# First stage of a decoder trunk: c as one row spread by TensorE, the square root's table behind the squares, whole modulation rows, diagonals scaled on ScalarE

## The chip, the cores and the metric

The kernel runs on one core of a Trainium2 chip. The metric is the device time of one execution in microseconds (us), as the median of several runs. PE is TensorE, DVE is VectorE, ACT is ScalarE, POOL is GpSimd; SP issues most of the DMAs and computes nothing. SBUF is the memory that the engines work on, PSUM the one that PE writes sums into.

## The reference

One layer of a hybrid decoder trunk on x (512 tokens, 1024 features). All its modulation vectors come from one vector c:

```python
cond = jax.nn.silu(c)
mod = (cond @ w_ada[l] + b_ada[l])[:, None, :]
sh1, sc1, g1, sh2, sc2, g2 = jnp.split(mod, 6, axis=-1)
h = _rms(x, norm1_w[l]) * (1 + sc1) + sh1
x = x + g1 * _hybrid_mixer(h, w_in[l], ...)
h = _rms(x, norm2_w[l]) * (1 + sc2) + sh2
x = x + g2 * (jnp.square(jax.nn.relu(h @ w_ff1[l])) @ w_ff2[l])
```

`_hybrid_mixer` multiplies h by `w_in` (queries, keys, values, state-space inputs, pooling inputs, gates), runs dilated window attention, a chunked state-space scan and a multi-scale pooling, projects and gates the three, and multiplies by `w_out`. `_rms` divides by the root of the mean square over the features.

## The kernel before

x is held transposed: `xT[k]`, k from 0 to 7, has 128 features on the partitions and 512 tokens along them. A float32 product of matrices is made as three matmuls (`mm3`, lines 287 to 289) of parts: every operand is a high part (`hh`, `wh`) rounded to fp32r, and a low part (`hl`, `wl`), the rest. The high part of a weight is a copy on ACT, the low part a subtraction on DVE.

The first stage, which the change rewrites, is in an order written out by hand for DVE, ACT, PE and SP: each engine runs its instructions in the order in which the code calls them. What follows after the k loop of this stage is ordered by a scheduler by priorities. The stage does this:

- SP loads c, broadcast to all 128 partitions (`crow`, two halves of 512), then the eight `xT`, with `vec` (all small vectors) behind the first and a constant behind the second, then rows of the modulation's weights (`ada_load(part, k)`: two DMAs of 128x512) and of the weights of queries and keys (`w_load`).
- ACT takes the silu of `crow`, loads the table of the square root (L359) and squares `xT` (L400, L401). DVE adds the squares in pairs (L405), all but the last pair; PE sums over partitions with a matrix of ones into `sx` (L403, L406). Meanwhile `warm` keeps PE running on ones (L394).
- DVE multiplies `sx` with the identity and sums (L416), so that each token's sum of squares comes to a partition; ACT takes a root, DVE the reciprocal and one Newton step (L421 to L426): r. Four diagonal matrices with r (L430) and a matmul with ones each (L431) spread r over partitions again, in PSUM.
- `dot(k, i, half)` is a modulation value as a product of a row of weights with `crow`, multiplied and summed by one DVE instruction (L368, in the trace with a read of the accumulator behind it); `dot_end` adds bias and norm weight (L374, L375, L377). i = 0 is the scale, i = 1 the shift; `bsc` is the bias plus one (L409).
- `high(k)` makes u = xT x scale x r (L453 for k = 0; ACT L450 and DVE L451 from k = 1) and hh = u + shift (ACT L454); `low(k)` makes hl (DVE L459). `by_residue` writes hh and hl in another order of tokens (ACT L445).
- A loop over k makes 24 matmuls of queries and keys with hh and hl of k, while DVE and ACT prepare k + 1. `w_high` (ACT L383) and `w_low` (DVE L387) split the weights.

All blocks of 128x512 come from one set of 59 places (`blk`, `free`). `background` holds the other 32 rows of the modulation, each computed later at a tick of the weight stream; they use `crow` too. The weights of the later stages come through `wstream`, whose raw, high and low blocks have pools of their own (`raws`, `wsp`).

Of the kernel before, what the change touches and what calls it, by code (L numbers as in the profile page):

```python
# [17 lines left out]
P = 128  # L18
D = 1024
T = 512  # L20
# [3 lines left out]
NBLK = 59  # L24
WARM = (18, 12, 6)
AHEAD = 300
# [72 lines left out]
def kernel(ctx: ExitStack, tc: tile.TileContext, a: dict, out: bass.AP, dbg=None):  # L99
# [41 lines left out]
    def small(shape, name, bufs=1, dt=F32):  # L141
        return sm.tile(shape, dt, tag=name, name=uid(name), bufs=bufs)
# [31 lines left out]
    vec = small([P, NVCOLS], "vec")  # L174
    small([P, 464], "gap")
    crow = [blk("crow") for _ in range(2)]
    xT = [blk(f"xT{k}") for k in range(8)]
# [76 lines left out]
    def tick(n=1):  # L254
        ticks[0] += 1
        for _ in range(n):
            if side:
                side.pop(0)()
        if ticks[0] % 2 == 0 and background:
            background.pop(0)()  # L260
            if not background:
                free(*crow)

# [69 lines left out]
    E = mybir.EngineType  # L333
    with tc.manual_schedule(engines={E.DVE, E.Activation, E.PE, E.SP}):
        for i in range(2):
            nc.sync.dma_start(crow[i], a["c"][:, i * T : (i + 1) * T].broadcast_to([P, T]))
        wt = {}

        def w_load(k):
            for ch in (Q, K):  # L340
                wt[ch, k] = blk("wst")
                nc.sync.dma_start(wt[ch, k], w_in[ch, k // 2][:, k % 2, :])

        for k in range(8):
            nc.sync.dma_start(xT[k], a["x"][k])
            if k == 0:
                nc.sync.dma_start(vec, a["vec"])
            if k == 1:
                nc.sync.dma_start(cst[:, :P], a["const"][:, :P])
        wa = [ada_load(1, 0)]  # L350
        wa.append(ada_load(0, 0))
        w_load(0)
# [3 lines left out]
        S.activation(junk1, epsc, AF.Silu)  # L356
        for i in range(2):
            S.activation(crow[i], crow[i], AF.Silu)
        S.activation(junk1, epsc, AF.Sqrt)  # L359
        A1 = [small([P, 2], f"A1{k}") for k in range(8)]  # L360
        bsc1 = small([P, 8], "bsc1")
        dots = {}

        def dot(k, i, half):
            if (k, i) not in dots:
                dots[k, i] = small([P, 2], "dot", 4)
            x = wa[i][half]
            V.scalar_tensor_tensor(x, x, 1.0, crow[half], ALU.mult, ALU.mult, accum_out=dots[k, i][:, half : half + 1])  # L368
            free(x)

        def dot_end(k, i):
            d, o = dots[k, i], A1[k][:, i : i + 1]
            if i == 0:
                V.scalar_tensor_tensor(o, d[:, 0:1], bsc1[:, k : k + 1], d[:, 1:2], ALU.add, ALU.add)  # L374
                V.tensor_tensor(o, o, vc("norm1_w", k), ALU.mult)  # L375
            else:
                V.scalar_tensor_tensor(o, d[:, 0:1], vc("b_ada", k), d[:, 1:2], ALU.add, ALU.add)  # L377

        wparts = {}
# [15 lines left out]

        warm(WARM[0])
        sp = psm("sx")
        for k in range(0, 8, 2):
            s0, s1 = blk("sq"), blk("sq")
            S.activation(s0, xT[k], AF.Square)  # L400
            S.activation(s1, xT[k + 1], AF.Square)  # L401
            if k == 6:
                mm(sp, lhsT=ones, rhs=s0, start=False, stop=False)  # L403
            else:
                V.tensor_tensor(s1, s0, s1, ALU.add)  # L405
            mm(sp, lhsT=ones, rhs=s1, start=(k == 0), stop=(k == 6))  # L406
            free(s0, s1)
            if k == 0:
                V.tensor_scalar(bsc1, vc("b_ada", 8, 8), 1.0, None, ALU.add)  # L409
        dot(0, 0, 0)  # L410
        dot(0, 0, 1)
        dot_end(0, 0)
        ss, var, rt, r, t = (small([P, 4], "rx" + n) for n in "svryt")
# [4 lines left out]
        S.activation(rt, ss, AF.Sqrt, scale=1.0 / D, bias=epsc)  # L418
        w_high(Q, 0)
        w_high(K, 0)  # L420
        V.tensor_scalar(var, ss, 1.0 / D, EPS, ALU.mult, ALU.add)  # L421
        dot(0, 1, 0)
        V.reciprocal(r, rt)
# [5 lines left out]
        for b in range(4):  # L429
            V.tensor_scalar(dg[b], ident, r[:, b : b + 1], None, ALU.mult)  # L430
            mm(rp[:, b * P : (b + 1) * P], lhsT=ones, rhs=dg[b], start=True, stop=True)  # L431
        warm(WARM[2])
        R1 = blk("R1")
        dot(0, 1, 1)
        dot_end(0, 1)
        hh = [cpool.tile([P, T], F32R, name=f"hh{k}", tag=f"hh{k}") for k in range(8)]
# [29 lines left out]
        low(0)  # L466
        w_low(K, 0)
        free(rp, wps)
        qps = [acc() for _ in range(4)]
        kps = [acc() for _ in range(4)]  # L470
        for k in range(8):
            if k < 7:
                wa = [ada_load(1, k + 1), ada_load(0, k + 1)]
                w_load(k + 1)
                dot(k + 1, 0, 0)
                if k:
                    low(k)
                dot(k + 1, 0, 1)
                w_high(Q, k + 1)
                w_high(K, k + 1)  # L480
                by_residue(1, k)
                dot(k + 1, 1, 0)
                dot_end(k + 1, 0)
                dot(k + 1, 1, 1)
                w_low(Q, k + 1)
                dot_end(k + 1, 1)
                high(k + 1, R1)
                w_low(K, k + 1)
# [800 lines left out]
```

## Time and profile before

| | us |
|---|---|
| median of 3 runs (1109.05 to 1109.62) | 1109.58 |
| the profiled execution | 1109.32 |
| span of the trace in it | 1107.5 |
| PE busy | 1098.5 |
| DVE busy | 597.1 |
| ACT busy | 507.5 |

The span goes from the first to the last instruction that the profile records; the profiled execution's own time is 1.8 us longer. TensorE's granted clock is shown as full almost everywhere. A row of the timeline names the start and the busy time of a group of equal instructions, the engine, the line, output and inputs, and in brackets how long the engine was idle before and what released it. Ends of matmuls are modelled, so a row of several matmuls is a little longer than their distance times their number.

### The profile page before, as it was taken

Reading aid. Unit: us, or ns where it says so; the run is one execution under the profiler, and the core shown is the slowest. Engines: PE = TensorE matmul, PEld = TensorE weight load, DVE = VectorE, ACT = ScalarE, POOL = GpSimd, SP = SyncE. Lnnn points to the kernel's source line nnn. Section 1 sums busy time; section 2 is a strip of 40 time slices with the busy share of each in tenths; the row PEclk is TensorE's granted clock in tenths of the full one; section 3 lists DMA queues with packets and bytes.
Section 4 is the critical chain, followed back from the end, with each engine's and each line's share of the span. In section 5 each row is a group of like instructions: output and inputs, shape, how many; then the busy total and the mean of one; then the engine's idle time right before and its main releaser. Section 6 shows DMA issues by size and latency. Waiting matters only on the chain.

```text
span 1107.5 us, 14079 instructions
## 1 busy us (share of the span) xinstructions
PE 1098.5 (99%) x5414; PEld 916.5 (83%) x5414; DVE 597.1 (54%) x1210; ACT 507.5 (46%) x953; POOL 0.2 (0%) x4
## 2 busy tenths in 40 slices
PE   8999999999999999999999999999999999999998
PEld 6878888888887888888888888899888888888887
DVE  6964773574766778478832433665544223455241
ACT  6895885643596456425422223343433122344120
POOL 0000000000000000000000000000000000000000
PEclk9999999999999999999999999999999999999999
DMA  9943343444543453322323432440133222222241
GB/s 337 314 141 106 115 157 100 133 134 130 186 130 96 125 163 121 119 83 77 123 96 124 143 95 96 142 163 2 60 105 100 96 95 95 96 96 95 95 133 38
DMA packets 49348, 134.45 MB, mean 121 GB/s; under 512 B 5617, under 2 KB 6385, under 8 KB 49281
## 3 DMA queue, kind: packets, MB, share of 16 engines
q1 hardware_dynamic: 47696, 130.81, 36.4%
q10 hardware_dynamic: 1584, 2.75, 0.8%
q8 instruction: 42, 0.69, 0.3%
q14 instruction: 26, 0.20, 0.1%
HBM read 131.41 MB, written 2.13 MB: 121 GB/s over the span
## 4 chain that ended last, share of the span: by engine, by line
PE 89%; ACT 4%; DMA 4%; DVE 2%; issue 1%; SPq 0%; ACTq 0%; DVEq 0%
PE psacc L287 27%; PE psacc L289 27%; PE psacc L288 27%; DMA wa<-in_w_ada_dram 1%; PE psS L566 1%; DMA M<-prow 1%; ACT wh L272 1%; PE psy L880 1%; PE pso L682 1%; PE psyo L888 1%; PE pso L680 1%; DVE conv L798 1%; DMA wst<-in_w_in_dram 0%; PE pskT L550 0%; PE pspT L663 0%
## 5 line engine op out<-in xcount | busy, mean ns | idle before, releaser
L273 DVE TENSOR_TENSOR wl<-raw,wh 128x1024 fp32r<-128x1024 f32 x161 | 196.9, 1223 | 335.5 <-ACT wh L272 333.9
L272 ACT CAST wh<-raw 128x1024 fp32r<-128x1024 f32 x161 | 168.9, 1050 | 365.5 <-PE psacc L288 321.4
L287 PE MATMUL psacc<-hl,wh 128*128 128x512 f32 x416 | 166.4, 400 | 0.6 <-ACT prev L843 0.5
L289 PE MATMUL psacc<-hh,wl 128*128 128x512 f32 x416 | 162.3, 390 | 0.0
L288 PE MATMUL psacc<-hh,wh 128*128 128x512 f32 x416 | 162.1, 390 | 0.0
L287 PEld LDWEIGHTS psacc<-hl,wh 128*128 128x128 f32 x416 | 78.2, 188 | 18.3 <-issue 1.2
L288 PE MATMUL psacc<-ah,wh 128*128 128x512 f32 (+1 forms) x242 | 92.1, 381 | 0.0
L288 PEld LDWEIGHTS psacc<-hh,wh 128*128 128x128 f32 x416 | 78.2, 188 | 16.8 <-issue 1.4
L287 PE MATMUL psacc<-al,wh 128*128 128x512 f32 (+1 forms) x242 | 92.1, 381 | 0.0
L289 PE MATMUL psacc<-ah,wl 128*128 128x512 f32 (+1 forms) x242 | 92.0, 380 | 0.0
L289 PEld LDWEIGHTS psacc<-hh,wl 128*128 128x128 f32 x416 | 78.1, 188 | 16.6
L288 PE MATMUL psacc<-gh,wh 128*128 128x512 f32 x224 | 87.2, 389 | 0.0
L287 PE MATMUL psacc<-gl,wh 128*128 128x512 f32 x224 | 87.2, 389 | 0.0
L289 PE MATMUL psacc<-gh,wl 128*128 128x512 f32 x224 | 87.0, 389 | 0.0
L287 PE MATMUL psacc<-wl,rh 128*128 128x512 f32 x192 | 77.1, 402 | 0.0
L289 PE MATMUL psacc<-wh,rl 128*128 128x512 f32 x192 | 75.2, 392 | 0.0
L288 PE MATMUL psacc<-wh,rh 128*128 128x512 f32 x192 | 74.9, 390 | 0.0
L237 DVE SCALAR_TENSOR_TENSOR wa<-wa,crow 128x512 f32<-128x512 f32 x64 | 43.3, 688 | 19.3 <-DMA wa<-in_w_ada_dram 19.0
L287 PEld LDWEIGHTS psacc<-al,wh 128*128 128x128 f32 x242 | 45.5, 188 | 8.9
L288 PEld LDWEIGHTS psacc<-ah,wh 128*128 128x128 f32 x242 | 45.5, 188 | 8.7
L289 PEld LDWEIGHTS psacc<-ah,wl 128*128 128x128 f32 x242 | 45.5, 188 | 8.7
L287 PEld LDWEIGHTS psacc<-gl,wh 128*128 128x128 f32 x224 | 42.1, 188 | 8.7
(350 smaller groups left out, 1955.8 us busy)
## 6 DMA issues: line engine op xcount, KB each, us to landing
raw<-in_w_in_dram SPq DMA_DIRECT2D x80, 512.0 KB, 3.5
raw<-in_w_ff_dram SPq DMA_DIRECT2D x64, 512.0 KB, 3.5
wa<-in_w_ada_dram SPq DMA_DIRECT2D x96, 256.0 KB, 4.1
wst<-in_w_in_dram SPq DMA_DIRECT2D x16, 256.0 KB, 5.4
M<-prow SPq DMA_DIRECT2D x16, 256.0 KB, 3.3
raw<-in_w_ssd_out_dram SPq DMA_DIRECT2D x8, 512.0 KB, 3.5
raw<-in_w_pool_out_dram SPq DMA_DIRECT2D x8, 512.0 KB, 3.4
raw<-in_w_out_dram SPq DMA_DIRECT2D x8, 512.0 KB, 3.5
```

The lines of the kernel that those rows point to most:

```text
L237: V.scalar_tensor_tensor(wa[i], wa[i], 1.0, crow[i], ALU.mult, ALU.mult, accum_out=d[:, i : i + 1])
L272: S.copy(wh, raw)
L273: V.tensor_tensor(wl, raw, wh.bitcast(F32), ALU.subtract)
L287: mm(ps, lhsT=wh, rhs=xl, start=first, stop=False)
L288: mm(ps, lhsT=wh, rhs=xh, start=False, stop=False)
L289: mm(ps, lhsT=wl, rhs=xh, start=False, stop=last)
L566: mm(so[b], lhsT=qT[:, b * P : (b + 1) * P], rhs=kT[:, (b + 1) * P - n : (b + 1) * P], start=True, stop=True)
L680: mm(od, lhsT=vs[kb][:, hs], rhs=pT[b // 2][:, cs : cs + P], start=(b == 0), stop=False, skip_group_check=True)
L682: mm(ov[:, b, :], lhsT=vs[b][:, hs], rhs=pT[0][:, b * P : (b + 1) * P], start=False, stop=(gi == 2 and b == 3), skip_group_check=True)
L798: V.scalar_tensor_tensor(t[:, i:], x[:, : T - i], cw[:, 3 - i, n : n + 1], t[:, i:], ALU.mult, ALU.add)
L880: mm(yp[half * 64 : half * 64 + 64, cs], lhsT=X[c][:, (2 * j + half) * 64 : (2 * j + half + 1) * 64], rhs=Ms[half][:, cs], start=True, sto ...
L888: mm(op[:, cs], lhsT=prev[c][:, j * P : (j + 1) * P], rhs=CT[:, cs], start=True, stop=True)
```

## The change

- c comes as two rows on one partition (`c1`), by DMAs on ACT's queue. ACT takes the silu of a row, PE spreads it with a matmul of one row of ones into PSUM, DVE copies it to `crow2`, which has a place of its own.
- SP issues all eight `xT` first, then `vec` and the constant, then whole rows of the modulation's weights (`ada_whole`, one DMA of 128x1024) into blocks that belong to `raws` and `wsp`.
- The table of the square root is loaded behind the squares. All four pairs of squares are added on DVE, so that there are four matmuls into `sx` instead of five. `bsc` stands ahead of the additions. There are 13 instead of 18 warming matmuls at the start.
- `dot(0, 0)` is put around the diagonals in two halves, `dot_end(0, 0)` and both halves of `dot(0, 1)` behind r. The diagonals are scaled on ACT (L441). The high parts of the first weights stand behind them.
- In the k loop a `dot` is one DVE instruction on 128x1024 and one that adds and multiplies. `high(k+1)` stands right behind `dot(k+1, 1)`, and both `w_low` behind that.

```diff
-WARM = (18, 12, 6)
+WARM = (13, 12, 6)
...
-    small([P, 464], "gap")
-    crow = [blk("crow") for _ in range(2)]
+    small([P, 432], "gap")
+    crow2 = small([P, 2, T], "crow")
+    crow = [crow2[:, i, :] for i in range(2)]
...
+        c1 = [blk("c1") for _ in range(2)]
         for i in range(2):
-            nc.sync.dma_start(crow[i], a["c"][:, i * T : (i + 1) * T].broadcast_to([P, T]))
+            nc.scalar.dma_start(c1[i][:1], a["c"][:, i * T : (i + 1) * T])
...
+        homes = [(raws, "raw"), (wsp, "wh"), (wsp, "wl")]
+
+        def ada_whole(part, k):
+            pool, tag = homes[0]
+            homes.append(homes.pop(0))
+            w = pool.tile([P, 2, T], F32, tag=tag, name=uid("wada"))
+            nc.sync.dma_start(w, a["w_ada"][part * 8 + k].rearrange("p (i t) -> p i t", i=2))
+            return w
+
         for k in range(8):
             nc.sync.dma_start(xT[k], a["x"][k])
-            if k == 0:
-                nc.sync.dma_start(vec, a["vec"])
-            if k == 1:
-                nc.sync.dma_start(cst[:, :P], a["const"][:, :P])
-        wa = [ada_load(1, 0)]
-        wa.append(ada_load(0, 0))
+        nc.sync.dma_start(vec, a["vec"])
+        nc.sync.dma_start(cst[:, :P], a["const"][:, :P])
+        wa = [ada_whole(1, 0), ada_whole(0, 0)]
         w_load(0)
...
-        for i in range(2):
-            S.activation(crow[i], crow[i], AF.Silu)
-        S.activation(junk1, epsc, AF.Sqrt)
...
+        def dot(k, i):
+            w, o, d = wa[i], A1[k][:, i : i + 1], small([P, 1], "dot1", 4)
+            V.scalar_tensor_tensor(w, w, 1.0, crow2, ALU.mult, ALU.mult, accum_out=d)
+            if i == 0:
+                V.scalar_tensor_tensor(o, d, bsc1[:, k : k + 1], vc("norm1_w", k), ALU.add, ALU.mult)
+            else:
+                V.tensor_tensor(o, d, vc("b_ada", k), ALU.add)
...
         warm(WARM[0])
+        cps = [psm("c") for _ in range(2)]
+        for i in range(2):
+            S.activation(c1[i][:1], c1[i][:1], AF.Silu)
+            mm(cps[i], lhsT=ones[:1], rhs=c1[i][:1], start=True, stop=True)
+            V.tensor_copy(crow[i], cps[i])
+        free(*cps, *c1)
+        V.tensor_scalar(bsc1, vc("b_ada", 8, 8), 1.0, None, ALU.add)
         sp = psm("sx")
...
-            if k == 6:
-                mm(sp, lhsT=ones, rhs=s0, start=False, stop=False)
-            else:
-                V.tensor_tensor(s1, s0, s1, ALU.add)
+            V.tensor_tensor(s1, s0, s1, ALU.add)
             mm(sp, lhsT=ones, rhs=s1, start=(k == 0), stop=(k == 6))
             free(s0, s1)
-            if k == 0:
-                V.tensor_scalar(bsc1, vc("b_ada", 8, 8), 1.0, None, ALU.add)
-        dot(0, 0, 0)
-        dot(0, 0, 1)
-        dot_end(0, 0)
+        S.activation(junk1, epsc, AF.Sqrt)
+        dot_half(0, 0, 0)
...
         S.activation(rt, ss, AF.Sqrt, scale=1.0 / D, bias=epsc)
-        w_high(Q, 0)
-        w_high(K, 0)
         V.tensor_scalar(var, ss, 1.0 / D, EPS, ALU.mult, ALU.add)
-        dot(0, 1, 0)
+        dot_half(0, 0, 1)
...
         for b in range(4):
-            V.tensor_scalar(dg[b], ident, r[:, b : b + 1], None, ALU.mult)
+            S.mul(dg[b], ident, r[:, b : b + 1])
             mm(rp[:, b * P : (b + 1) * P], lhsT=ones, rhs=dg[b], start=True, stop=True)
         warm(WARM[2])
+        dot_end(0, 0)
+        dot_half(0, 1, 0)
+        dot_half(0, 1, 1)
+        dot_end(0, 1)
+        w_high(Q, 0)
+        w_high(K, 0)
         R1 = blk("R1")
-        dot(0, 1, 1)
-        dot_end(0, 1)
...
         low(0)
-        w_low(K, 0)
...
             if k < 7:
-                wa = [ada_load(1, k + 1), ada_load(0, k + 1)]
+                wa = [ada_whole(1, k + 1), ada_whole(0, k + 1)]
                 w_load(k + 1)
-                dot(k + 1, 0, 0)
+                dot(k + 1, 0)
                 if k:
                     low(k)
-                dot(k + 1, 0, 1)
+                else:
+                    w_low(K, 0)
                 w_high(Q, k + 1)
                 w_high(K, k + 1)
                 by_residue(1, k)
-                dot(k + 1, 1, 0)
-                dot_end(k + 1, 0)
-                dot(k + 1, 1, 1)
+                dot(k + 1, 1)
+                high(k + 1, R1)
                 w_low(Q, k + 1)
-                dot_end(k + 1, 1)
-                high(k + 1, R1)
                 w_low(K, k + 1)
```

How the instructions stand is shown at three places. The first is DVE from its first work to the diagonals. Before (qkw is a small vector for a later stage, dot a partial product):

```order
L502 TENSOR_SCALAR qkw_737<-vec_76 128x1
L405 TENSOR_TENSOR sq_156<-sq_155,sq_156 128x512
L409 TENSOR_SCALAR bsc_33_134<-vec_76 128x8
L405 TENSOR_TENSOR sq_163<-sq_162,sq_163 128x512
L405 TENSOR_TENSOR sq_169<-sq_168,sq_169 128x512
L368 SCALAR_TENSOR_TENSOR wa_107,dot_180<-wa_107,crow_78 128x512
L368 SCALAR_TENSOR_TENSOR wa_108,dot_180<-wa_108,crow_79 128x512
L374 SCALAR_TENSOR_TENSOR A_25_126<-dot_180,bsc_33_134 128x1
L375 TENSOR_TENSOR A_25_126<-A_25_126,vec_76 128x1
L416 SCALAR_TENSOR_TENSOR diag_50_190,rxs_185<-pssx_154,cst 128x128
```

The same stretch of DVE after the change:

```order
L413 COPY crow_78<-psc_143 128x512
L413 COPY crow_78<-psc_144 128x512
L415 TENSOR_SCALAR bsc_32_128<-vec_76 128x8
L421 TENSOR_TENSOR sq_154<-sq_153,sq_154 128x512
L421 TENSOR_TENSOR sq_160<-sq_159,sq_160 128x512
L421 TENSOR_TENSOR sq_166<-sq_165,sq_166 128x512
L421 TENSOR_TENSOR sq_172<-sq_171,sq_172 128x512
L373 SCALAR_TENSOR_TENSOR wada_108,dot_178<-wada_108,crow_78 128x512
L514 TENSOR_SCALAR qkw_686<-vec_76 128x1
L429 SCALAR_TENSOR_TENSOR diag_51_185,rxs_180<-pssx_152,cst 128x128
```

bsc, which reads `vec`, moved from behind the first addition to ahead of all of them; a fourth addition came in, and one half of a dot stands ahead of the diagonals instead of two with their ends.

The second place is DVE from hl(0) to hl(1). Before:

```order
L459 SCALAR_TENSOR_TENSOR hl_250<-u_77_274,A_25_126,hh_242 128x512
L387 TENSOR_TENSOR wsl_203<-wst_117,wsh_202 128x512
L368 SCALAR_TENSOR_TENSOR wa_290,dot_302<-wa_290,crow_78 128x512
L368 SCALAR_TENSOR_TENSOR wa_291,dot_302<-wa_291,crow_79 128x512
...
L387 TENSOR_TENSOR wsl_306<-wst_298,wsh_305 128x512
L377 SCALAR_TENSOR_TENSOR A_26_127<-dot_312,vec_76 128x1
L451 TENSOR_TENSOR u_98_319<-u_98_319,R_60_239 128x512
L387 TENSOR_TENSOR wsl_309<-wst_300,wsh_308 128x512
L368 SCALAR_TENSOR_TENSOR wa_349,dot_361<-wa_349,crow_78 128x512
L459 SCALAR_TENSOR_TENSOR hl_251<-u_98_319,A_26_127,hh_243 128x512
```

After:

```order
L474 SCALAR_TENSOR_TENSOR hl_248<-u_78_272,A_24_120,hh_240 128x512
L385 SCALAR_TENSOR_TENSOR wada_287,dot_91_295<-wada_287,crow_78 128x1024
L387 SCALAR_TENSOR_TENSOR A_25_121<-dot_91_295,bsc_32_128,vec_76 128x1
L399 TENSOR_TENSOR wsl_237<-wst_114,wsh_236 128x512
L385 SCALAR_TENSOR_TENSOR wada_289,dot_96_306<-wada_289,crow_78 128x1024
L389 TENSOR_TENSOR A_25_121<-dot_96_306,vec_76 128x1
L466 TENSOR_TENSOR u_97_309<-u_97_309,R_61_239 128x512
L399 TENSOR_TENSOR wsl_300<-wst_291,wsh_299 128x512
L399 TENSOR_TENSOR wsl_303<-wst_293,wsh_302 128x512
L385 SCALAR_TENSOR_TENSOR wada_340,dot_102_348<-wada_340,crow_78 128x1024
L387 SCALAR_TENSOR_TENSOR A_26_122<-dot_102_348,bsc_32_128,vec_76 128x1
L474 SCALAR_TENSOR_TENSOR hl_249<-u_97_309,A_25_121,hh_241 128x512
```

Between u(1) and hl(1) there stood one subtraction and half a dot; now there are two subtractions, a whole dot and its end. Ahead of u(1) there is one subtraction less.

The third place is ACT behind the k loop, where the scheduler's order begins (ea is an exponential for the state-space part, wd a small cast). Before:

```order
L272 CAST wh_854<-raw_852 128x1024
L731 CAST wd_887<-wdt_885 128x8x16
L272 CAST wh_892<-raw_890 128x1024
L324 COPY q_739<-psacc_282 128x512
L324 COPY q_740<-psacc_283 128x512
```

After:

```order
L271 CAST wh_803<-raw_801 128x1024
L743 CAST wd_836<-wdt_834 128x8x16
L271 CAST wh_841<-raw_839 128x1024
L271 CAST wh_899<-raw_897 128x1024
L323 COPY q_688<-psacc_279 128x512
L783 ACT_TABLE_LOAD
L783 ACTIVATE ea_987<-hv_89 128x16
L323 COPY q_689<-psacc_280 128x512
```

A load of the exponential's table came in between the first two copies of queries, and a third cast ahead of them.

## Rows read from the trace of the kernel before

**Rows 1.** The page's first part: busy time, share, instructions of each engine.

```profile
PE 1098.5 (99%) x5414; PEld 916.5 (83%) x5414; DVE 597.1 (54%) x1210; ACT 507.5 (46%) x953; POOL 0.2 (0%) x4
```

**Rows 2.** Waits of PE, 30 us to the end: total, times, longest (us).

```profile
PE psacc L287 <- ACT prev L843: 0.5, 1, 0.5
```

**Rows 3.** Stretches: length, busy PE PEld DVE ACT POOL, clock, DMA, GB/s.

```profile
0.00:20.20 20.20, 16.09 (x90) 12.51 (x90) 9.59 (x37) 10.70 (x19) 0.20 (x4) 1.00 0.92 323
...
28.00:66.00 38.00, 38.00 (x169) 31.44 (x168) 37.38 (x107) 32.98 (x48) 0.00 (x0) 1.00 0.86 288
```

**Rows 4.** Timeline to the diagonals: start, busy, engine, line.

```profile
0.73 0.86 SPq L336 DMA_DIRECT2D crow<-in_c_dram  x2
...
1.07 5.91 PE L394 MATMUL pswarm<-ones 128*128 128x128 f32 x36 [1.07 <-DVE ones L354]
...
4.51 0.63 ACT L358 ACTIVATE crow<-crow 128x512 f32<-128x512 f32 x1 [2.29 <-DMA crow<-in_c_dram]
...
8.80 0.69 DVE L405 TENSOR_TENSOR sq<-sq,sq 128x512 f32<-128x512 f32 x1 [2.06 <-ACT sq L401]
...
9.55 3.30 PE L406 MATMUL pssx<-sq,ones 128*128 128x512 f32 x6 [2.57 <-DVE sq L405]
...
12.69 1.02 PE L403 MATMUL pssx<-sq,ones 128*128 128x512 f32 x2
...
13.54 1.02 PE L406 MATMUL pssx<-sq,ones 128*128 128x512 f32 x2
...
14.60 0.29 DVE L416 SCALAR_TENSOR_TENSOR diag<-pssx,cst 128x128 f32<-128x128 f32 x1 [0.52 <-PE pssx L406]
```

**Rows 5.** PE by line, 2.0 to 3.0 us, then 5.0 to 5.5.

```profile
L394 PE MATMUL pswarm<-ones 128*128 128x128 f32 x7 | 1.7, 421 | 0.0
...
L394 PE MATMUL pswarm<-ones 128*128 128x128 f32 x7 | 0.9, 275 | 0.0
```

**Rows 6.** Short stretches of the start, columns as in rows 3.

```profile
2.00:2.50 0.50, 0.50 (x4) 0.50 (x3) 0.00 (x0) 0.21 (x2) 0.00 (x0) 1.00 0.83 184
...
4.50:5.00 0.50, 0.50 (x6) 0.50 (x6) 0.00 (x0) 0.49 (x1) 0.00 (x0) 1.00 1.10 247
...
8.00:9.00 1.00, 0.00 (x0) 0.00 (x0) 0.20 (x1) 1.00 (x4) 0.00 (x0) 1.00 1.06 406
```

**Rows 7.** One tile: the DMAs of xT, issue to landing; last issue at 6.6.

```profile
L345 SPq DMA_DIRECT2D xT<-in_x_dram x8: 328/427/437, 1.6 to 6.6; - x8
...
DMA to landing us min/median/max: 4.6/4.7/5.0
```

**Rows 8.** Timeline from the scaled diagonals to the second stall.

```profile
17.06 0.88 DVE L430 TENSOR_SCALAR diag<-cst,rxy 128x128 f32<-128x128 f32 x4
...
18.71 0.74 DVE L453 SCALAR_TENSOR_TENSOR u<-xT,A,psrx 128x512 f32<-128x512 f32 x1
...
19.49 0.72 ACT L454 ACTIVATE hh<-u,A 128x512 fp32r<-128x512 f32 x1 [2.59 <-DVE u L453]
...
20.26 0.50 PE L287 MATMUL psacc<-wsl,hh 128*128 128x512 f32 x1 [0.37 <-ACT hh L454]
...
22.74 0.69 DVE L368 SCALAR_TENSOR_TENSOR wa<-wa,crow 128x512 f32<-128x512 f32 x1
...
23.35 0.22 DVE L374 SCALAR_TENSOR_TENSOR A<-dot,bsc 128x1 f32<-128x1 f32 x1
...
23.81 0.72 ACT L450 ACTIVATE u<-xT,A 128x512 f32<-128x512 f32 x1
...
26.84 0.75 DVE L459 SCALAR_TENSOR_TENSOR hl<-u,A,hh 128x512 fp32r<-128x512 f32 x1
...
27.64 0.50 PE L289 MATMUL psacc<-wsh,hl 128*128 128x512 f32 x1 [0.39 <-DVE hl L459]
```

**Rows 9.** Timeline of DVE: an instruction on 128x1024.

```profile
61.91 1.23 DVE L273 TENSOR_TENSOR wl<-raw,wh 128x1024 fp32r<-128x1024 f32 x1 [0.17 <-ACT wh L272]
```

**Rows 10.** Timeline of ACT, and the chain of the heads' part.

```profile
79.49 1.28 ACT L771 ACT_TABLE_LOAD   x1
...
311.37 1.19 ACT M L870 x4
```

More of the change, by code (lines that the diff above doesn't have):

```diff
@@ L260, in tick @@
             background.pop(0)()
-            if not background:
-                free(*crow)
     def flush():
@@ L362, with dot_half @@
         dots = {}
-        def dot(k, i, half):
+        def dot_half(k, i, half):
             if (k, i) not in dots:
                 dots[k, i] = small([P, 2], "dot", 4)
-            x = wa[i][half]
+            x = wa[i][:, half, :]
             V.scalar_tensor_tensor(x, x, 1.0, crow[half], ALU.mult, ALU.mult, accum_out=dots[k, i][:, half : half + 1])
-            free(x)
         def dot_end(k, i):
```

## Prediction

> **What bounds the kernel now.** I read the shares of the engines first. PE is busy for 1098.5 of the 1107.5 us, 99% [rows 1]. The longest entry in its list of waits from 30 us to the end is 0.5 us, at line 843 [rows 2]. So the time is the length of a product stream that nothing can shorten here, plus what PE loses before the stream runs freely. The stretch up to 20.2 us shows that loss: PE's 16.09 us there are warming and small matmuls, DMA is busy for 92%; from 28 us PE is busy all the time [rows 3]. The question is therefore narrow: at what moment does the stream start, how often does it stall, and does anything late in the program take back what is won.
>
> Next I followed the start by the timeline [rows 4]. The two broadcast copies of c are issued first, then x, with vec behind its first row. Every pair of squares is added on DVE, the sum goes into one of the matmuls of the sum of squares, and the first of these starts at 9.55. PE had stood still for 2.57 us. The last one ends at about 14.56 (a row of two from 13.54, 1.02), DVE's diagonals start at 14.60. The part from r to the first product is in [rows 8]: DVE scales four diagonals (17.06), writes u (18.71), ACT writes hh (19.49), the first product starts at 20.26. The second k has two more stalls: hl(1), written from 26.84, is what PE waits for until 27.64.
>
> **The start: DMA.** The broadcast of c is two times 256 KB. From 2.0 to 2.5 us, the first traffic, it has the queues to itself, at 184 GB/s [rows 6]. After the change c is two single rows, on ACT's queue, and x is first. x is 8 x 262 KB = 2.1 MB. From 8 us, where broadcasts are gone, the stream shows 406 GB/s [rows 6]; I take 390, since neighbours vary. First data moved 1.3 us after the first issue (0.73, so 2.0). 2.0 + 2.1/0.39 = 7.4 is the last byte. A landing is seen later: the last x was issued at 6.6 and took 5.0 [rows 7], so 11.6, about 1.0 behind its bytes. x is complete at 8.4; if it starts as slowly as 247 GB/s, a stretch in [rows 6], and holds that for some time, it is nearer 9.8. vec is 77 KB behind it: 8.8, bounds 8.6 to 10.05. The first whole row of the modulation, 512 KB, follows at about 10.4 (to 11.6), before the diagonals need DVE. c itself does not gate: even the broadcast was in SBUF when the silu ran at 4.51 [rows 4].
>
> **The start: PE.** Warming is 18 fp32 matmuls, 36 records, in 5.91 us [rows 4]. Seven records make 1.7 us of busy time in a stretch early and 0.9 later [rows 5], about 0.24 and half of that each; 14 slow and 22 fast ones fill the 5.91, so the pace changed near 1.07 + 14 x 0.236 = 4.4 us. Thirteen are 26 records, 14 slow and 12 fast, ending at 5.8. Two matmuls with c then take 0.85 each (from 12.69 to 13.54, two records, [rows 4]) and end at 7.5. DVE copies them out of PSUM at the 0.74 of u, which also reads PSUM [rows 8], until 8.3. This lies under the wait for vec, at nothing; were c late by more than 0.5 us, it would cost from there.
>
> **From vec to the diagonals.** bsc stands ahead of the additions now, and it waits for vec (the first place in the order). Behind it on DVE are all four additions, and behind these the matmuls. bsc 8.8, the first addition from 9.0, 0.69 each [rows 4], the first matmul at 9.75, four at 0.853: the last ends at 13.33 with its tail, diagonals from 13.37. That is **1.23 us earlier** than 14.60. The bounds: vec at 8.4 gives 1.85, vec at 10.05 gives nothing.
>
> **From r to the first product.** ACT scales a 128x128 with one factor per row at 1.19/4 = 0.30 us [rows 10], DVE at 0.88/4 = 0.22 [rows 8]. From the first scaled diagonal to u it was 18.71 - 17.06 = 1.65 before. Now the four go to ACT, and DVE meanwhile ends dot(0,0) and does both halves of dot(0,1): 0.33 and 2 x 0.69 (the halves of [rows 8]) and 0.13, near 1.8. ACT's 4 x 0.30 with the last diagonal's matmul and its way to DVE, some 0.6, is 1.8 too. I take 1.8: **0.15 later**. Bounds 1.65 and 2.0. First product: 20.26 - 1.23 + 0.15 = 19.2.
> The Trainium skill ("ScalarE: Activation LUTs", Rules for kernel authors) says of a plain multiplication to use VectorE and not ScalarE. The rows agree by size, 0.30 against 0.22; but DVE is freed of four instructions that ACT does beside it, and by the rule alone one would book 0.3 us of loss where the sum above books 0.15.
>
> **The second k.** Count from the start of hh(0). Before: hl(1) starts at 26.84 - 19.49 = 7.35. After, DVE's row (second place in the order) is hl(0) to 1.5, dot(1,0) whole, its end, w_low(K,0), dot(1,1), its end, then u(1). A 128x1024 subtraction is 1.23 [rows 9]; less the 0.08 by which a half dot is overlapped (22.74 + 0.69 is 23.43, the next row starts at 23.35, [rows 8]) a whole dot is 1.15. Its end, which waits for the dot's result, I put at 0.26 (0.22 in [rows 8], and the wait); 1.41 in all. DVE is at about 5.0 there, and ACT's part of u ends at 24.53 - 19.49 = 5.04 (23.81 + 0.72, [rows 8]), so u starts at 5.09, 0.44 earlier than before. Behind u, however, stand both w_low (0.6 each), dot(2,0) with its end (1.41), and only then hl(1): 5.09 + 0.60 + 1.2 + 1.41 = **8.30**, 0.95 later than before. PE needs hl(1) after its first two products of k=1, so it gets it 0.95 later relative to the start: most of the gain is handed back here. Net at the end of this stall: 1.08 - 0.95 = 0.13 gained. From then on PE needs 24 x 38.00/169 = 5.40 for a k [rows 3], where it was never idle and DVE was busy for 37.38 of 38.00. DVE's period after is 2 x 1.41 + 0.69 + 0.75 + 1.0, near 5.3. No further stall, and none gone. The bounds: nothing handed back if PE's backlog covers it (it doesn't: PE already waited here), 1.3 if the whole dots take the 1.23 of the subtraction in full.
>
> **Later.** ACT loads one table more: exp comes in between the copies of q, sqrt goes back behind it, and exp comes again before dte (third place in the order). Before there was one, 1.28 us at 79.49 [rows 10]. I book 0.3 us of PE waiting (nothing at best, 1.28 if PE stands for a whole load). The heads' masks move to an emptier stretch of ACT, which can remove the 0.5 us wait of [rows 2]: -0.5, bounds -0.5 and 0. Warming: five fewer, beside waits, at nothing. Pools: 16 whole rows now lie in the buffers of the weight stream, of which the first block in the rows is split at 61.91 [rows 9], at nothing.
> The Trainium skill ("ScalarE: Activation LUTs", What ACT_TABLE_LOAD costs) gives a switch 1283 ns and a drain of about 1380. The load agrees with 1.28; by the page the one load more would cost 2.66, and the sum would be 2.4 higher if none of it were hidden.
>
> **The sum.** -0.13 - 0.2 = -0.33 against the profiled run of 1109.32 (span 1107.5 and 1.8 around it): 1109.0. That run lies 0.26 below the median of 1109.58, so against the median 1109.2. **I predict 1109.2 us**, no change that a measurement of this kernel can tell (about 0.2%, 2.2 us).
>
> **The rivals.**
> A, the forecast: the gain of the start is handed back by hl(1). 1108.2 to 1110.2. For it: PE's stall until 27.64 is the last wait of the start, and DVE's row grows ahead of it. 58%.
> B, the gain stays: vec lands at 8.4, or whole dots are shorter than I sum. -1.85 + 0.15, 0 to 0.5 handed back, late 0 to -0.5: -2.2 to -1.2, so 1107.4 to 1108.4, and down to 1106.8 if the stall until 27.64 shrinks too. Against it: DVE's row ahead of hl(1) only grew. 18%, somewhat over half of it under 1107.4.
> C, slower: PE's clock falls. The two matmuls with c use one row of the array; if they don't hold the clock, PE stands from 5.8 to 9.75 as far as that goes, 3.9 us against the 2.57 that it bore before at full pace. The four matmuls would take 2 x 0.853 each, +3.4, or half of it if the pace returns on the way, as it did at the start. It decides from the point where the pause is longer than the one that [rows 4] shows to be harmless. 1110.7 to 1112.6. 10%, two thirds of it over 1111.8. In the profile it is matmuls of the sum of squares 1.7 apart.
> The Trainium skill ("TensorE: Matmul & The Clock Gate", What's actually happening) calls the throttled state the default that activity lifts, 1.2 against 2.4 GHz; [rows 5] show it at the start; whether matmuls of one row lift it, no row shows.
> D, a table load hits PE: +1.3 near 63 or 92 us: 1110.2 to 1111.8. Against it: the longest entry of PE's list [rows 2] is at another place. 10%.
> E, the start isn't earlier, since vec and the whole rows land late: +0.95 remains, 1110.1. 4%.
>
> **The numbers.** Faster by over 0.2%: 10%, from B. Slower: C's 7% and 1% of D. The range 1107.3 to 1111.3 leaves out some 8% below and 10% above; it takes in vec's bounds (-0.6, +1.2), the dots' (+0.35) and the table's (+1.0), which are not all at their ends together.
>
> **What would show it.** Diagonals at 13.4; first product at 19.2; hl(1) starting 8.3 us after hh(0) and PE waiting for it near 28; the matmuls of the sum of squares 0.85 apart (C); a wait on copies of q or on dte (D). Wrong it would be if whole dots took far from 1.41 with their ends, or if vec landed before x.

## The result: 5 us slower, and the profile after

The changed kernel takes 1114.91 us, the median of 4 runs (1113.65 to 1115.67), against 1109.60 of the kernel before beside it. The ratio is 1.0048 with a 95% interval of 1.0035 to 1.0060. The prediction was 1109.2 in a range of 1107.3 to 1111.3, with 8% for slower. The profiled execution is the slowest of the four, 1115.67, with a span of 1113.9.

The page's first part after (columns as in [rows 1]):

```profile
PE 1102.9 (99%) x5406; PEld 917.0 (82%) x5406; DVE 598.2 (54%) x1174; ACT 512.2 (46%) x958; POOL 0.2 (0%) x4
```

PE's busy time grew by 4.4 us with eight records fewer. Some 2.9 of it is work at a lower clock (the sum of squares, below). The other 1.5 are small gaps in the loop over k that the page counts as busy, since the modelled ends of the matmuls fill them: the list of waits shows none of them (from 31.10 to 66.00 PE counts as busy for 34.74 of 34.90 us). The other 2 us of the span are waits. PE's list of waits over the whole span, after (us in total, times, longest; it answers to [rows 2] and to the waits in [rows 4] and [rows 8]):

```profile
PE pssx L422 <- DVE sq L421: 2.1, 1, 2.1
PE psacc L288 <- DVE hl L474: 1.8, 1, 1.8
PE psrr L214 <- DVE diag L213: 1.3, 1, 1.3
...
PE psacc L286 <- DVE ol L314: 0.4, 1, 0.4
```

The timeline of the start after, from the warming to the first product (it answers to [rows 4] and [rows 8]):

```profile
1.08 5.36 PE L406 MATMUL pswarm<-ones 128*128 128x128 f32 x26 [1.08 <-DVE ones L362]
...
6.37 1.98 PE L412 MATMUL psc<-c,ones 1*128 1x512 f32 x4
...
9.63 0.17 DVE L415 TENSOR_SCALAR bsc<-vec 128x8 f32<-128x8 f32 x1 [0.55 <-DMA vec<-in_vec_dram]
...
10.45 6.42 PE L422 MATMUL pssx<-sq,ones 128*128 128x512 f32 x8 [2.10 <-DVE sq L421]
...
16.90 0.29 DVE L429 SCALAR_TENSOR_TENSOR diag<-pssx,cst 128x128 f32<-128x128 f32 x1 [3.96 <-PE pssx L422]
...
21.21 0.75 DVE L468 SCALAR_TENSOR_TENSOR u<-xT,A,psrx 128x512 f32<-128x512 f32 x1
...
21.99 0.72 ACT L469 ACTIVATE hh<-u,A 128x512 fp32r<-128x512 f32 x1 [0.33 <-DVE u L468]
...
22.77 0.50 PE L286 MATMUL psacc<-wsl,hh 128*128 128x512 f32 x1 [0.25 <-ACT hh L469]
```

The four matmuls of the sum of squares take 6.42 us for eight records, where four at 0.853 would take 3.4. The stretches around them show the granted clock (the column ahead of the DMA share):

```profile
8.50:9.00 0.50, 0.00 (x0) 0.00 (x0) 0.50 (x1) 0.44 (x2) 0.00 (x0) 1.00 1.13 436
9.00:9.50 0.50, 0.00 (x0) 0.00 (x0) 0.08 (x1) 0.44 (x2) 0.00 (x0) 0.61 1.03 413
9.50:10.00 0.50, 0.00 (x0) 0.00 (x0) 0.37 (x2) 0.50 (x1) 0.00 (x0) 0.50 0.99 393
...
14.00:15.00 1.00, 1.00 (x3) 0.46 (x2) 0.00 (x0) 0.00 (x0) 0.00 (x0) 0.50 0.99 391
15.00:16.00 1.00, 1.00 (x3) 0.48 (x2) 0.00 (x0) 0.00 (x0) 0.00 (x0) 0.53 1.04 389
16.00:17.00 1.00, 1.00 (x5) 0.52 (x5) 0.10 (x1) 0.00 (x0) 0.00 (x0) 1.00 1.08 416
```

It fell from full (2.4 GHz) to half (1.2 GHz) near 9.1, while PE stood still behind the two matmuls with c, and rose near 15.9. In the kernel before it never left 1.00 here, over a pause of 2.57 us [rows 4]. The diagonals start at 16.90 instead of 14.60 and the first product at 22.77 instead of 20.26.

The second part is the loop over k. PE waits 1.78 us for hl(1) (the second entry of the list, and 31.11 below), and then falls behind by a third of a microsecond in each of the next five k. One round of the loop after, DVE and ACT from one hl to the next, with the product on PE that takes each hl and the one ahead of the second:

```profile
30.30 0.75 DVE L474 SCALAR_TENSOR_TENSOR hl<-u,A,hh 128x512 fp32r<-128x512 f32 x1
...
31.08 1.13 ACT L460 CAST rl<-hl 128x512 fp32r<-128x512 f32 x1 [0.33 <-DVE hl L474]
31.11 0.50 PE L288 MATMUL psacc<-wsh,hl 128*128 128x512 f32 x1 [1.78 <-DVE hl L474]
...
32.12 0.72 ACT L465 ACTIVATE u<-xT,A 128x512 f32<-128x512 f32 x1
...
32.88 0.69 DVE L466 TENSOR_TENSOR u<-u,R 128x512 f32<-128x512 f32 x1 [0.48 <-ACT u L465]
33.48 1.29 DVE L399 TENSOR_TENSOR wsl<-wst,wsh 128x512 fp32r<-128x512 f32 x2
...
34.69 1.22 DVE L385 SCALAR_TENSOR_TENSOR wada<-wada,crow 128x1024 f32<-128x1024 f32 x1
...
35.95 0.22 DVE L387 SCALAR_TENSOR_TENSOR A<-dot,bsc,vec 128x1 f32<-128x1 f32 x1
36.09 0.75 DVE L474 SCALAR_TENSOR_TENSOR hl<-u,A,hh 128x512 fp32r<-128x512 f32 x1
...
36.49 0.39 PE L287 MATMUL psacc<-wsh,hh 128*128 128x512 f32 x1
...
36.89 0.50 PE L288 MATMUL psacc<-wsh,hl 128*128 128x512 f32 x1
```

This is a ring. hl goes to a copy on ACT (rl); behind the copy, in ACT's row, stands u; DVE adds to u, then does both subtractions of weights, a whole dot and its end, and then the next hl. Each step waits for the one before: ACT idles 0.33 for hl, DVE 0.48 for u, in every round. The ring takes 36.09 - 30.30 = 5.79 us, longer than the 5.4 to 5.46 that PE needs for a k, though neither DVE nor ACT is full. It runs five times, from hl(1) to hl(6); in the last k there is no next dot, and hl(7) comes 4.40 behind hl(6). On PE the products that take an hl are 36.89 - 31.11 = 5.78 apart.

The third part is late, at the norm of the state-space part:

```profile
418.30 1.22 DVE L272 TENSOR_TENSOR wl<-raw,wh 128x1024 fp32r<-128x1024 f32 x1
...
419.81 0.69 DVE L238 SCALAR_TENSOR_TENSOR wa<-wa,crow 128x512 f32<-128x512 f32 x1 [0.30 <-DMA wa<-in_w_ada_dram]
...
420.43 0.17 DVE L191 RECIPROCAL rr4y<-rr4r 128x4 f32<-128x4 f32 x1
...
421.57 0.71 PE L214 MATMUL psrr<-diag,ones 128*128 128x128 f32 x4 [1.35 <-DVE diag L213]
```

The scheduler put the reciprocal behind a split of weights and a half dot of a later modulation row, whose DMA was late. PE waits 1.35 us.

**The account of the profiled execution.** Up to the first product: +2.51 (22.77 - 20.26). hl(1) is 0.96 later relative to hh(0) (8.31 against 7.35), so PE's stall ends +3.47 (31.11 - 27.64). Five further rounds of 5.79 against 5.46: +1.65, so that the loop ends (at the first product with rh, which follows it) +5.18 (70.61 - 65.43). The wait of [rows 2] is gone: -0.5. The norm: +1.1. The wait for ol, of which the list before has no entry: +0.4. That makes +6.2 of the +6.4 in the span. The end of the loop before, then after:

```profile
65.43 0.39 PE L287 MATMUL psacc<-wl,rh 128*128 128x512 f32 x1
```

```profile
70.61 0.39 PE L286 MATMUL psacc<-wl,rh 128*128 128x512 f32 x1
```

### The profile page after: what moved, and what is told of

Its sections match the earlier page's. It is cut to its first block, busy times and chain, and to the rows that moved or that the text cites. A ratio compares the mean times of both kernels' runs of the same rounds, so it can differ in the third digit from the quotient of the medians.

```text
span 1113.9 us, 14017 instructions
## 1 busy us (share of the span) xinstructions
PE 1102.9 (99%) x5406; PEld 917.0 (82%) x5406; DVE 598.2 (54%) x1174; ACT 512.2 (46%) x958; POOL 0.2 (0%) x4
## 4 chain that ended last, share of the span: by engine, by line
PE 93%; DVE 2%; ACT 2%; DMA 2%; SPq 0%; issue 0%; ACTq 0%; DVEq 0%
PE psacc L286 28%; PE psacc L288 28%; PE psacc L287 28%; PE psS L578 1%; PE psy L892 1%; PE pssx L422 1%; DMA wa<-in_w_ada_dram 1%; PE psyo L900 1%; DMA M<-prow 1%; PE pso L692 1%; PE pso L694 0%; PE psst L851 0%; DMA vec<-in_vec_dram 0%; PE pskT L562 0%; PE pspT L675 0%; ACT sqj L523 0%
```

## The experiments

Two theories for the clock were put against each other: (1) the matmuls of one row don't hold it, so PE's pause counts from the end of the warming; (2) only the standstill behind them counts. For the loop there was the ring.

**e1: 18 warming matmuls in the changed kernel.**

```diff
-WARM = (13, 12, 6)
+WARM = (18, 12, 6)
```

> The changed kernel with 18 instead of 13 warming matmuls at the start. Warming then ends near 7.0 instead of 6.4 us, the two matmuls with c near 8.9, the sum of squares still starts near 10.45. Theory 1 (matmuls of one row do not hold the clock, so the pause counts from the end of the warming): the pause is 3.4 us, the clock still falls, near 9.7, and the four matmuls take about 6.2 us; the time is 1114 to 1115. Theory 2 (only the standstill behind the matmuls with c counts, 2.1 us in the changed kernel): it is 1.5 us here, the clock stays, the four matmuls take 3.4 us, and the time falls by 2.8 to about 1112.

Measured: 1113.79 (1112.11 to 1114.33), ratio 1.0039 (1.0024 to 1.0053). The mean granted clock of the whole execution was 0.997 or 0.998 in all four runs; it was 1.000 in most runs of the kernel before, so the clock fell somewhere in each of the four. In the profiled one the sum of squares ran at full pace, and the clock fell at the other pause, behind the wait for hl(1). Stretches and timeline of this kernel:

```profile
29.00:30.00 1.00, 1.00 (x4) 0.86 (x5) 1.00 (x1) 1.00 (x1) 0.00 (x0) 0.95 1.03 406
30.00:31.00 1.00, 1.00 (x4) 0.71 (x4) 0.47 (x4) 0.75 (x2) 0.00 (x0) 0.50 1.02 401
```

```profile
29.00 0.50 PE L288 MATMUL psacc<-wsh,hl 128*128 128x512 f32 x1 [1.77 <-DVE hl L474]
...
30.57 0.63 PE L287 MATMUL psacc<-wsh,hh 128*128 128x512 f32 x1
```

This did not decide between the theories, since each execution shows a fall at another place. It showed that the clock can fall behind the second pause too (near 29.9, when PE had been back at work for 0.9 us), and that products then start 0.43 apart instead of 0.23.

**e2: the same two matmuls with c over 128 rows, 127 of them zeros (the zeros and the ones are written first).**

```diff
+            V.memset(c1[i], 0.0)
...
-            mm(cps[i], lhsT=ones[:1], rhs=c1[i][:1], start=True, stop=True)
+            mm(cps[i], lhsT=ones, rhs=c1[i], start=True, stop=True)
```

> The changed kernel with the two matmuls that spread c made over 128 rows, of which 127 hold zeros (the blocks of c are set to zero first); number, place and length of the matmuls are the same. Theory 1 (one row does not hold the clock): the granted clock stays full until the sum of squares, its matmuls are 0.85 apart, the diagonals start near 14.0 instead of 16.9, the time falls by about 2.8 to 1112. Theory 2 (the standstill of 2.1 us behind them decides): the clock falls near 9.1 as before, diagonals near 16.9, no change from 1114.9.

Measured: 1113.92 (1113.17 to 1114.13), ratio 1.0041 (1.0026 to 1.0056). The profiled execution (1113.17) has full clock from end to end, with a pause of 2.08 us ahead of the sum of squares, as long as the one in which the clock had fallen, and diagonals at 14.54. The three others have a mean clock of 0.997 or 0.998, so the gain of 2.8 did not come in the median. What theory 1 forecast came in one execution of four; where the clock fell in the others, no trace shows.

**e3: hl(k) ahead of the dot in the loop.**

```diff
-                dot(k + 1, 0)
                 if k:
                     low(k)
-                else:
+                dot(k + 1, 0)
+                if not k:
                     w_low(K, 0)
```

> The changed kernel with hl(k) ahead of the dot(k+1,0) in the loop over k, from k = 1. Theory (a ring hl - copy on ACT - u on ACT - u on DVE - two subtractions - a whole dot and its end - next hl takes 5.79 us against PE's 5.46, and the dot stands between u(1) and hl(1)): without the dot in it the ring is 4.4, DVE's period falls to about 5.3, PE's stall at hl(1) shrinks from 1.8 to about 0.4 and no k after it loses 0.33; the time falls by 1.4 + 1.9 = 3.3 to 1111.6. Rival (DVE has no slack, so the dot is late instead and u waits for it): u(k+1) comes 1.4 later, the period stays 5.8, no change.

Measured: 1111.62 (9 runs, 1110.62 to 1112.69), ratio 1.0020 (1.0010 to 1.0030). The 3.3 us came in full (3.1 by the ratios). PE's wait for hl(1) is 0.4 in its list of waits, and u comes in a steady period of 5.33 to 5.35, DVE's own sum. Waits of PE, the timeline of DVE, and PE's first product, in this kernel:

```profile
PE psacc L288 <- DVE hl L474: 0.4, 1, 0.4
```

```profile
26.00 0.69 DVE L466 TENSOR_TENSOR u<-u,R 128x512 f32<-128x512 f32 x1 [0.25 <-ACT u L465]
...
31.33 0.69 DVE L466 TENSOR_TENSOR u<-u,R 128x512 f32<-128x512 f32 x1
```

```profile
21.67 0.50 PE L286 MATMUL psacc<-wsl,hh 128*128 128x512 f32 x1 [0.26 <-ACT hh L469]
```

From the first product to the end of the loop (66.38) it takes 44.71 us here, 47.84 in the changed kernel and 45.17 in the kernel before. So 3.1 us of the loss belong to the place of this one dot, whatever the clock does at the start. The mean clock was below 0.999 in all nine runs.

**e4: six warming matmuls behind those with c.**

```diff
         free(*cps, *c1)
+        warm(6)
```

> The changed kernel with six warming matmuls more, behind the two matmuls with c. They fill 8.35 to about 9.8 us of the pause. Theories 1 and 2 alike: the clock stays full, the sum of squares takes 3.4 instead of 6.2 us, diagonals near 14.0, the time falls by 2.8 to about 1112. If it does not fall, neither the rows nor the standstill decides, and the fall has another cause.

Measured: 1115.13 (1113.58 to 1116.87), ratio 1.0054 (1.0039 to 1.0069). The time did not fall, against what both theories said. The stretches of this kernel show why:

```profile
7.00:8.00 1.00, 1.00 (x4) 0.20 (x2) 0.69 (x1) 0.98 (x3) 0.00 (x0) 1.00 1.00 381
8.00:9.00 1.00, 1.00 (x8) 1.00 (x8) 0.69 (x1) 0.95 (x2) 0.00 (x0) 0.75 1.14 380
9.00:10.00 1.00, 1.00 (x6) 1.00 (x6) 0.60 (x2) 0.92 (x3) 0.00 (x0) 0.50 1.04 406
```

PE is busy without a gap here, and the clock falls near 8.5, right behind the two matmuls of one row (6.07 to 8). So a standstill isn't needed, which speaks against theory 2: the one-row matmuls were followed by a fall with no pause behind them. Theory 1 as it was put, a pause counted from the end of the warming, doesn't sort the traces either: e1 kept its clock at the start over 3.4 us counted that way (7.70 to 11.06), and here it fell 2.4 us behind the warming (6.15 to 8.5), with full matmuls running again. What sets the moment of a fall stays open; b1 below shows that little work at full pace ahead goes with a fall as well. In this execution the clock was back near 11.9, the diagonals start at 14.78, and the time is 1113.58, the lowest of the four.

**e5: e2 and e3 together.** 

> The changed kernel with both edits: c spread by matmuls over 128 rows (127 of zeros) and hl(k) ahead of the dot in the loop over k. If the two act apart: the run of the full rows at full clock (1113.2) less the 3.3 of the loop, 1109.9, with the mean clock at 1.0 in most runs. If matmuls of one row have no part in the falls of the clock: as hl(k) first alone, 1111.6 with mean clocks of 0.998.

Measured: 1109.99 (10 runs, 1109.29 to 1111.64), ratio 1.0011 (1.0002 to 1.0021). The mean clock is 1.0 in eight of ten runs; with one row (e3) it was in none of nine. The pause ahead of the sum of squares is 2.43 here, longer than in e3 (1.46), where the clock fell:

```profile
10.36 3.70 PE L424 MATMUL pssx<-sq,ones 128*128 128x512 f32 x8 [2.43 <-DVE sq L423]
```

e3 and e5 differ in the rows of these matmuls and in what the zeros need, so the pair shows that in this kernel 128 rows keep the clock far more often than one. They were not measured beside each other, but the kernel before had full clock in 11 of 12 runs beside e3 and in 26 of 31 beside e5, so the series themselves do not explain it. Rows are not all of it: e2, with 128 rows and the loop as changed, kept the clock in one run of four, which fits the fall behind the wait for hl(1) that e1 shows. The two parts of the loss are 3.1 to 3.3 for the ring and 1.0 to 1.6 for the clock (the ratios differ by 0.0009, the medians by 1.6).

**b1 and b2: the kernel before with 13 warming matmuls, and with two one-row matmuls behind them.**

```diff
-WARM = (18, 12, 6)
+WARM = (13, 12, 6)
...
         warm(WARM[0])
+        rows = blk("rows")
+        V.memset(rows[:1], 1.0)
+        for _ in range(2):
+            mm(wps, lhsT=ones[:1], rhs=rows[:1], start=True, stop=True)
+        free(rows)
```

The lines from `rows` on are in b2 alone.

> The kernel before with 13 instead of 18 warming matmuls and nothing else. PE's pause ahead of the sum of squares grows from 2.6 to about 3.2 us, which nothing waits for. If the pause alone makes the clock fall: most runs show a mean clock of 0.997 to 0.998, the sum of squares slows, the time rises by 1 to 3 us. If not: 1109.3, as before.

> The kernel before with 13 warming matmuls and behind them two matmuls of one row with 512 columns (of ones, into the warming's place, read by nothing). They end near 8.1, the pause behind them is 1.5 us. If matmuls of one row hold the clock: no falls, 1109.3, also where 13 alone falls. If they do not: as 13 alone, or with more falls, since the warming ends at the same moment.

Measured: b1 1110.23 (10 runs, 1109.69 to 1111.62), ratio 1.0010 (1.0000 to 1.0019); b2 1111.25 (10 runs, 1110.51 to 1112.11), ratio 1.0017 (1.0007 to 1.0026). The mean clock is under 0.999 in all ten runs of either, and 0.999 or more in 26 of the 31 runs of the kernel before beside them. So taking away the five matmuls that the prediction let go at nothing brings the fall by itself, and costs about 1 us (the interval reaches down to no change), and one-row matmuls in the pause don't help. b1's warming and its sum of squares:

```profile
1.08 5.80 PE L394 MATMUL pswarm<-ones 128*128 128x128 f32 x26 [1.08 <-DVE ones L354]
9.41 4.54 PE L406 MATMUL pssx<-sq,ones 128*128 128x512 f32 x6 [2.53 <-DVE sq L405]
```

The pause is as long as before, 2.53, and the clock fell; my expectation named the longer pause as the reason, and in this execution it wasn't longer. What is shorter is the work at full pace ahead of it: 26 records in 5.80 ran mostly at half pace, while 36 filled 5.91 before [rows 4].

**e8: the squares first, with the loop of e3.** The additions no longer wait for vec, and the first two stand ahead of the copies of c; the first matmul of the sum stands ahead of the two with c; bsc stands behind the additions.

> The changed kernel with hl(k) ahead of the dot in the loop, and the start in another order: the additions of the squares do not wait for vec any more, the first two stand ahead of the copies of c, the first matmul of the sum of squares ahead of the two with c, bsc behind all additions. PE then has work from 1.1 to about 12 us without a pause over 1 us. Expected at full clock: diagonals near 12.3 (16.9 in the changed kernel, 14.6 before), the first product near 18.2 (22.8, 20.3), and with the wait of 1.2 at the norm of the state-space part still there 1108.3; rival: the data or the dots of k = 1 are late then and PE stalls at the first products: 1110.

Measured: 1108.80 (10 runs, 1107.53 to 1109.87), ratio 0.9996 (0.9987 to 1.0005). Five of the ten runs have a mean clock of 0.999 or more, and take 1107.53 to 1108.51; the others take 1109.10 to 1109.87. Diagonals start at 13.23 in the profile, not 12.3, since the copies of c hold the third addition back.

**e9: a higher priority for the norm's chain in the changed kernel.**

```diff
-        rr = token_rsqrt(st["sums", g], T, "rr")
+        with tc.high_priority(offset=AHEAD + 100):
+            rr = token_rsqrt(st["sums", g], T, "rr")
```

> The changed kernel with a higher priority, for the scheduler, of the small chain that makes the norm of the state-space part (sum, root, reciprocal, Newton step, diagonals) and nothing else. In the changed kernel PE waits 1.3 us for its diagonals, since the reciprocal stands behind a split of weights and a half dot whose DMA is late on DVE. Theory (the place in DVE's row is the cause): the wait falls to 0.2 to 0.4, the time by about 1, to 1113.9. Rival (DVE has no slack there, whatever the order): something else waits as long, 1114.9.

Measured: 1114.88 (1114.80 to 1115.17), ratio 1.0050 (1.0035 to 1.0065). Nothing gained. The wait for the diagonals is gone from PE's list, and another stands there, for the sum that the chain starts from:

```profile
PE psrr L202 <- DVE sums L224: 0.8, 1, 0.8
```

**e10, e11, e12: a start that keeps the clock.** e10 is e8 with c over 128 rows; e11 is e10 with the priority of e9; e12 is e10 with the copies of c between the additions and the silu behind the first pair of squares.

> The kernel with the squares first and hl(k) first (1108.8, clock at 1.0 in five of ten runs), and c spread by matmuls over 128 rows. Theory (only one-row matmuls leave a hole in PE's work that the clock sees): the mean clock is 1.0 in nearly all runs, the time that of the five, 1108.0. Rival (the falls there have another cause): half of the runs at 0.998 again, 1108.8.

> As the kernel with the squares first over 128 rows, and the higher priority for the norm's chain. If the parts act apart: 1108.0 less 0.7 to 1.0, 1107.2, 2 us under the kernel before; if the priority only moves the wait: 1108.0.

> The kernel with the squares first over 128 rows, with the silu of c behind the first pair of squares on ACT, both spreading matmuls behind the second sum, and the two copies of c between the additions on DVE. The copies stood ahead of the last two additions (diagonals 13.82); now the last addition ends near 10.9, the sum of squares near 11.8, diagonals near 12.4. If the rest of the chain moves along: 1.4 less than 1109.1, 1107.7, at full clock. Rival: the first products then wait for something that did not gate (weights of k = 0, PE at hl(1)), and the time stays at 1109.

Measured: e10 1109.08 (10 runs), ratio 0.9997 (0.9987 to 1.0007); e11 1109.07 (10 runs), ratio 1.0000 (0.9991 to 1.0009); e12 1108.21 (11 runs, 1107.50 to 1109.08), ratio 0.9992 (0.9983 to 1.0001). The mean clock is 1.0 in all 31 runs of the three. e8 and e10 are a second pair that differs in the rows and the zeros: full clock in five of ten runs with one row, in ten of ten with 128. e10 lost against e8 what the clock gave: the zeros make c later, and diagonals start at 13.82. e11 shows again that the priority doesn't pay. In e12 the first product starts 1.3 us ahead of that in [rows 8]:

```profile
13.11 0.29 DVE L437 SCALAR_TENSOR_TENSOR diag<-pssx,cst 128x128 f32<-128x128 f32 x1
...
18.96 0.50 PE L286 MATMUL psacc<-wsl,hh 128*128 128x512 f32 x1 [0.25 <-ACT hh L477]
```

Its list of waits still has 1.3 us at the norm, and the median lies 0.7 (by the ratio 0.9) below that of the kernel before. It is the fastest of the versions, but its interval just includes no change, so that it beats the kernel before is not shown.

## Why the prediction was wrong, point by point

- **Warming, "five fewer, beside waits, at nothing", and the matmuls with c "at nothing".** This is one of the two steps that failed. Both were costed by PE's time, and PE had time; what they do to the clock stood in rival C alone and was no term of the sum. b1 gives the price of the five alone, about 0.0010 of the time, 1.1 us; e3 against e5 gives that of the one row, 1.0 to 1.6. The two don't add: with 128 rows behind the thirteen matmuls the clock held in eight of ten runs (e5). In the profiled execution the fall cost 2.9 at the sum of squares (6.25 us from 10.45 to the next warming at 16.70, against 3.4). Rival C described the mechanism, with the matmuls 1.7 apart (6.25/4 = 1.56 here), and had 10%; its 1110.7 to 1112.6 was passed because the ring came on top. That one-row matmuls may not hold the clock could not be read from the trace of before.
- **The moment of the rise, 4.4 us.** It was taken as fixed. 26 records filled 5.36 us here, which by the same arithmetic is 19 or 20 at half pace, a rise near 5.7; PE finished with c at 8.35 instead of 7.5.
- **vec at 8.8.** bsc ran at 9.63, inside the bounds (8.6 to 10.05). The stream of x did not run at 390 GB/s from the first byte (147 from 2.0 to 2.5 us, 205 from 4.0 to 4.5). So even at full clock the diagonals come at 14.10 (e5) to 14.54 (e2), a gain of 0.1 to 0.5 and not of 1.23. The largest gain that it allowed was also wrong by its own steps: vec at 8.4, which lies under the bound of 8.6, gives 1.63 and not 1.85.
- **r to the first product, 0.15 later.** From the diagonals to u it is 21.21 - 16.90 = 4.31 against 18.71 - 14.60 = 4.11: 0.20. Right.
- **hl(1) 8.30 behind hh(0).** 30.30 - 21.99 = 8.31. Right, and with it the 0.95 handed back.
- **"No further stall".** Wrong, by 1.65 us (five rounds), and the second step that failed. The step compared DVE's period (near 5.3) with PE's need, found it shorter, and stopped. DVE's sum was right in its total: e3 runs at 5.33 (its 1.0 for the two subtractions was 1.2 some lines above, and is 1.21 in the trace). But a period is also bounded by the longest ring through several engines, and all its members but the copy rl had been priced in the paragraph above. From the start of one to the start of the next they are: hl 0.78, rl 1.04, u 0.76, u on DVE 0.60, two subtractions 1.21, dot and end 1.40, together 5.79. They were never added up. e3 shows that the ring is the cause: with the dot out of it, these gaps are gone.
- **The table loads, 0.3 us and rival D.** The load between the copies of q is there, and no entry of PE's list stands between 32 and 110 us:

```profile
69.10 1.28 ACT L783 ACT_TABLE_LOAD   x1
```

  So the load was hidden: rival D did not come, and the 0.3 that was booked was not paid. The Trainium skill ("ScalarE: Activation LUTs", What ACT_TABLE_LOAD costs) gives a switch a drain on top of the load; the 2.4 us that the prediction estimated from it did not come either.
- **The wait of [rows 2].** It is gone, as forecast. In its place came 1.3 us at the norm (0.2 before), which no step foresaw. e9 and e11 show that moving the chain up only moves the wait. What in the change brought it is open: the scheduler's order behind the first stage differs in many places, but with the same split and half dot ahead of the reciprocal the changed kernel, e1, e2, e3 and e4 show 1.3, 0.4, 1.1, 1.8 and 1.3.

The sum of the prediction was -0.33. Put right with what was measured it is: diagonals -0.1 to -0.5, r to u +0.2, hl(1) +0.96, ring +1.65, clock +1.0 to +2.9, waits late +0.6 to +1.0, so 4 to 6.6 us. Measured: 5.3.

## What to carry to other kernels

Where engines hand work round in a loop, add up the ring from one instruction back to itself, over all engines, and compare that with the bound; the busy sum of each engine isn't enough. Warming matmuls and matmuls that happen to run in a pause do two jobs, and one taken away "at nothing" has to be priced by what the clock does without it. Here matmuls that spread one row over 128 partitions kept PE occupied without keeping it at full clock; with zeros in the other rows it stayed there in most runs (e5) or in all (e10).

## What the runs showed of the hardware that was not expected

- Matmuls of one row of 512 columns did not hold the granted clock: 0 of 9 runs at full mean clock with one row (e3), 8 of 10 with 128 rows and a longer pause behind (e5), 0 of 10 against 26 of 31 in the kernel before (b2, though b1, without them, has 0 of 10 as well). With full matmuls ahead of them and behind, five of ten with one row (e8) became ten of ten with 128 (e10). In e4 the clock fell to half while PE had no gap at all. The Trainium skill ("TensorE: Matmul & The Clock Gate", What's actually happening) ties the gate to how busy PE has been recently; by that rule alone, with busy as the profile shows it, the stretch in e4 would have kept the clock, and the trace differs.
- The first rise of the clock is not at a fixed time of the program: 26 warming records fill between 4.97 (e11) and 5.92 us (e2, e3), and 36 fill 5.91 in the kernel before [rows 4] and 6.62 in e1.
- Which pause brings the fall differs between executions of nearly the same code (the clock falls near 9.1 in the changed kernel, near 29.9 in e1). What it costs differs too: in e3 it fell near 10.4 and was back near 13.8, and the diagonals start at 15.80 instead of 16.90.
